# The attention's gate made token major, ahead of the other gate, and multiplied before the transposes

## The chip, the cores and the metric

One core of one Trainium2 chip runs the whole program. The time is the device time of one execution in microseconds (us). The engines are TensorE (PE in the profile, its weight loads PEld), VectorE (DVE), ScalarE (ACT), GpSimd (POOL) and SyncE (SP), whose queue issues every DMA of this kernel.

## The reference

One layer of a hybrid decoder trunk for 1024 tokens of width 1024, all in float32:

```python
z = rms_norm(h, mix_norm) @ w_in
q, k, v, gate_a, u, gate_s = split(z, 512 columns each)
attn = dilated_mixture_attention(q, k, v) * silu(gate_a)     # 8 heads of 64
ssm  = s5_glu(u, ...) * silu(gate_s)                         # 32 groups of 16 channels
h = h + concat(attn, ssm) @ w_out
h = h + sigmoid(rms_norm(h, ple_norm) @ w_g) * (p @ w_p)
```

The norm's gain is folded into x (`xh`, `xl`), and its factor per token, 1/rms, is applied where a projection leaves PSUM.

## The kernel before, in words

x is held feature major (channels on partitions, tokens along the row), `xh[k]` and `xl[k]` for the eight k tiles of 128 channels. Each float32 product is made of three matmuls of a high and a low part (`mm3`, lines 107 to 109): hi by hi, hi by lo, lo by hi. A weight tile of 128x512 is loaded by `load_w` (152), its high part is made by ScalarE (157) and its low part by VectorE or GpSimd (158). There are eight buffers for high parts and eight for low parts (`nbuf=8`), so the weights of one section of `w_in` replace those of the section before it as its last matmuls are done, and three buffers for raw tiles.

1/rms is there in two forms: `rrow`, spread over partitions and running along the row (for feature-major results), and `rcol`, one column per block of 128 tokens (for token-major results).

The work in order: u (six tiles, then two), the statistics, the state space heads (`ssm_kernels`, `ssm_scan`, `ssm_out`, `ssm_store`, lines 497 to 614), the two gates (632 to 642), q and k (694 to 731), then v, the attention, the GLU and half of the output projection, woven into each other by `step` (842), which runs the generator `attention` (754) on by one or two heads at a time, then the attention's half of the output projection and the embedding gate. The order of the instructions on each engine isn't that of the source: a list scheduler lays them out at build time by priority and by estimated durations and due times. `tc.high_priority` moves a block ahead. In the run each engine and the SP queue take their instructions strictly in that order. The gates' matmuls thus lie between those of the state space heads.

**The gates before.** For gate_s (columns 2560 on), then for gate_a (1536 on), eight weight tiles are loaded, and `feat_tile` (450) makes eight feature-major tiles of 128 channels by 512 tokens in the two `big` banks of PSUM, 24 matmuls each. VectorE multiplies a tile by `rrow` out of PSUM (640), ScalarE applies SiLU in place (641), SP stores it (642) into `sg_s` or `sa_s` in DRAM, both [512, 1024] feature major.

**The end of an attention block before** (`output`, 757 to 767). The attention's result for the 128 tokens of block b is `atok`, token major, evicted by VectorE (835) into one of two buffers (`wa`). `output(b)` loads the gate's 128 channels by 4 by 128 tokens into `gl` (tile `ga`, one buffer: `GA = 1`, line 760), transposes `atok` by four matmuls with the identity into a `t` bank (763; two such banks), multiplies by the gate on VectorE out of PSUM into `gl` (764), and splits that (`split`, 735 to 737) into a high part `mah` on ScalarE and a low part `mal` on GpSimd (`EA = "QQ"`, Q is GpSimd). `gl` comes free when the low part is done. The blocks 0, 1, 4 and 5 are held back (`HOLD`): their `output` is written down with that of block 2 and of block 6. `mah` and `mal` take buffers that the GLU's inputs held, so the first of them can be written only when the GLU is nearly done.

`tok_tiles` (648) makes token-major tiles (128 tokens by 512 channels; x is the stationary operand, w the moving one), before for q, k and v only.

Of the kernel before, what the change touches and what calls it, by code (L numbers as in the profile page):

```python
# [15 lines left out]
OP = mybir.AluOpType  # L16
# [61 lines left out]
def hybrid_layer(ctx: ExitStack, tc: tile.TileContext, a: dict, dbg=None):  # L78
# [22 lines left out]
    sg_s = dr.tile([512, S], F32, name="sg_s")  # L101
    sa_s = dr.tile([512, S], F32, name="sa_s")
    yg_s = dr.tile([512, S], F32, name="yg_s")
# [20 lines left out]

# [1 line left out]
    wp = ctx.enter_context(tc.tile_pool(name="wp", bufs=4, side="right"))  # L126
# [106 lines left out]

# [1 line left out]
    def p16(name):  # L235
# [136 lines left out]

    # powers of A: PA = [Re; -Im], PB = [-Im; -Re]
    pa, pb = named("pa", (P, G, 9)), named("pb", (P, G, 9))
# [43 lines left out]

    # rotations e^{i 8 theta k}, k = 16 a + b; sine rows are [s; -s]
    e1c, e1s = csr, snr  # L420
# [37 lines left out]
    def ev(name, shape=(P, 512)):  # L458
        return rp.tile(list(shape), F32, tag="ev", name=name, bufs=4)
# [171 lines left out]

# [1 line left out]
    for c0, dst in ((2560, sg_s), (1536, sa_s)):  # L633
        w = [load_w(wp, a["w_in"], k, c0, lo=GL) for k in range(KT)]
        for f in range(4):
            for n in range(2):
                o = feat_tile(w, f, n, "big", f"g{c0}{f}{n}")
                gt_ = ev(f"gate{c0}{f}{n}")
                with tc.high_priority(offset=AHEAD):
                    V.tensor_tensor(gt_, o, rrow[:, n * 512:(n + 1) * 512], op=OP.mult)  # L640
                    A.activation(gt_, gt_, AF.Silu)
                nc.sync.dma_start(dst[f * P:(f + 1) * P, n * 512:(n + 1) * 512], gt_)

    rrp.close()

# [1 line left out]
    kvp = ExitStack()  # L647
    def tok_tiles(w, bs, names, tag):
# [5 lines left out]
        return os_  # L654

    at = kvp.enter_context(tc.tile_pool(name="at", bufs=1))
    ph2 = ExitStack()
# [36 lines left out]
    for which, c0 in (("q", 0), ("k", 512)):  # L694
        w = [load_w(wp, a["w_in"], k, c0) for k in range(KT)]
        for bp in range(4):
# [19 lines left out]
            for b in (2 * bp, 2 * bp + 1):  # L716
# [10 lines left out]
                else:  # L727
# [3 lines left out]
                    nc.sync.dma_start(ks[:, :, c], hl, transpose=True)  # L731
# [1 line left out]
    ma, ms_ = {}, {}  # L733
# [20 lines left out]
    def attention():  # L754
        held = []

        def output(b):
            n, at_ = b // 4, atok.pop(b)
            gl = b3[0].tile([P, 4, P], F32, tag="ga", name=f"ga{b}", bufs=GA)
            nc.sync.dma_start(gl, sa_s.rearrange("(r p) t -> p r t", p=P)[:, :, b * P:(b + 1) * P])  # L760
            tp = bank("t", f"at{b}").rearrange("p (r t) -> p r t", t=P)
            for j in range(4):
                T.transpose(tp[:, j], at_[:, j], ident)
            tt(gl, tp, gl, OP.mult)
            if n not in ma:
                ma[n] = quad(f"mah{n}"), quad(f"mal{n}")
            split(*(t_[:, b % 4] for t_ in ma[n]), gl.rearrange("p r t -> p (r t)"), E[EA[b % 2]])

# [107 lines left out]

# [1 line left out]
    rawp[0] = ctx.enter_context(tc.tile_pool(name="raw2", bufs=RAW[1], side="right"))  # L878
# [43 lines left out]

# [1 line left out]
    def out_proj(part, src, scale, done):  # L924
# [124 lines left out]
def _w_in_columns():  # L1049
    """The u section with the channels of a group ahead of its groups."""  # L1050
    n = np.arange(3072)
    n[2048:2560] = n[2048:2560].reshape(4, 8, 16).transpose(0, 2, 1).reshape(512)
    return n
# [72 lines left out]
```

## Time and profile before

| | |
|---|---|
| time, median of 3 runs | 690.49 us (690.44 to 690.92) |
| span of the profiled execution, first to last instruction | 686.2 us |
| own time of the profiled execution | not given; the median lies 4.3 us above its span |
| mean granted TensorE clock | 0.968 |
| busy: PE, DVE, ACT, POOL | 630.0, 496.8, 289.5, 302.0 us |
| chain that ended last | PE 46%, DVE 26%, DMA 12%, issue 7%, ACT 5% |

A share over the whole span is a mean over stages with different limits. The stages here: u and the statistics to about 62 us, the state space heads with the gates' matmuls between them from 62 to 222 us, q, k and v to about 376, attention with GLU and output projection to 520, and the dense end. In the timeline an item's busy time may overlap the next one's; the distance of the starts is what an instruction takes out of its engine's time.

### The profile page before, as it was taken

How to read it: one execution, taken by the hardware profiler on the slowest of the kernel's cores; microseconds unless marked ns; L12 is line 12 of the kernel's file. 1: busy time of each engine (PE TensorE's matmuls, PEld its weight loads, DVE VectorE, ACT ScalarE, POOL GpSimd, SP SyncE). 2: the span in 40 equal slices, each digit the busy share in tenths (PEclk: the TensorE clock that was granted, in tenths of full speed). 3: DMA queues.
4: the chain of work that ended last, by engine and by line, in shares of the span. 5: the costliest groups of instructions: out<-in, count | busy, mean ns of one | idle time of the engine just before them, and what ended most of it. 6: DMA issues, size and time to landing. Idle time of an engine off the chain costs nothing.

```text
span 686.2 us, 10942 instructions
## 1 busy us (share of the span) xinstructions
PE 630.0 (92%) x3836; PEld 491.9 (72%) x3836; DVE 496.8 (72%) x1126; ACT 289.5 (42%) x553; POOL 302.0 (44%) x230
## 2 busy tenths in 40 slices
PE   9997799777879999999899789889999999999997
PEld 6875577566768788877677556566677888888786
DVE  6999999899998557767553998957944766626322
ACT  7532123445576624348434646534513455113100
POOL 3433825866775224234332845422432437342641
PEclk9999899998999999999999889989999999999999
DMA  7803612323444746754661868899987243015101
GB/s 257 241 7 109 209 38 76 105 79 93 77 92 92 167 69 125 159 86 125 161 122 48 216 147 148 213 192 191 217 226 244 94 152 124 15 63 165 50 32 61
DMA packets 158119, 87.25 MB, mean 127 GB/s; under 512 B 117232, under 2 KB 130416, under 8 KB 158064
## 3 DMA queue, kind: packets, MB, share of 16 engines
q1 hardware_dynamic: 158064, 86.56, 50.7%
q8 instruction: 30, 0.49, 0.3%
q14 instruction: 25, 0.20, 0.1%
HBM read 48.81 MB, written 17.27 MB: 96 GB/s over the span
## 4 chain that ended last, share of the span: by engine, by line
PE 46%; DVE 26%; DMA 12%; issue 7%; ACT 5%; POOL 2%; SPq 1%; DVEq 0%; ACTq 0%; POOLq 0%
PE gt L108 4%; PE gt L109 4%; PE gt L107 3%; DMA wr<-in_w_in 3%; DMA pt<-hl 3%; PE oa L107 2%; PE oa L109 2%; PE oa L108 2%; DVE tmp L270 2%; PE q L109 2%; PE q L107 2%; PE q L108 2%; DVE wl L158 2%; DVE p L780 2%; PE k L108 2%
## 5 line engine op out<-in xcount | busy, mean ns | idle before, releaser
L158 POOL TENSOR_TENSOR wl<-wr,wh 128x512 fp32r<-128x512 f32 x34 | 49.4, 1457 | 67.8 <-ACT wh L157 44.5
L157 ACT ACTIVATE wh<-wr 128x512 fp32r<-128x512 f32 x68 | 41.9, 626 | 51.4 <-DMA wr<-in_w_in 22.4
L810 POOL TENSOR_TENSOR hl<-p,hl 128x384 f16<-128x384 f32 (+2 forms) x34 | 38.9, 1148 | 53.9 <-ACT hl L807 27.1
L107 PE MATMUL g<-xh,wh 128*128 128x512 f32 x128 | 52.6, 411 | 7.3 <-DVE gate L640 5.5
L109 PE MATMUL g<-xh,wl 128*128 128x512 f32 x128 | 52.5, 410 | 5.3 <-DVE wl L158 5.3
L803 ACT ACTIVATE p<-p,st 128x384 f32<-128x384 f32 (+4 forms) x64 | 39.8, 622 | 39.1 <-DVE st L780 38.9
L108 PE MATMUL g<-xl,wh 128*128 128x512 f32 x128 | 52.0, 407 | 0.0
L108 PE MATMUL gt<-hl,wh 128*128 128x512 f32 (+1 forms) x136 | 51.7, 381 | 0.0
L107 PE MATMUL gt<-hh,wh 128*128 128x512 f32 (+1 forms) x136 | 51.7, 382 | 0.0
L109 PE MATMUL gt<-hh,wl 128*128 128x512 f32 (+1 forms) x136 | 51.2, 382 | 0.0
L158 DVE TENSOR_TENSOR wl<-wr,wh 128x512 fp32r<-128x512 f32 x34 | 34.8, 1025 | 19.1 <-ACT wh L157 14.0
L1016 ACT ACTIVATE gg<-gg 128x512 f32<-128x512 f32 (+1 forms) x17 | 10.1, 605 | 67.4 <-DVE gg L270 67.2
L1018 POOL TENSOR_TENSOR gg<-gg,hs 128x512 f32<-128x512 f32 x14 | 18.0, 1290 | 43.1 <-DVE gg L270 41.5
L107 PEld LDWEIGHTS g<-xh,wh 128*128 128x128 f32 x128 | 24.6, 192 | 13.7 <-DVE gate L640 6.5
L270 DVE TENSOR_TENSOR gg<-gt,rrow 128x512 f32<-128x512 f32 (+1 forms) x17 | 10.8, 656 | 32.7 <-PE gt L109 32.6
L109 PEld LDWEIGHTS g<-xh,wl 128*128 128x128 f32 x128 | 24.7, 193 | 12.0 <-DVE wl L158 6.6
L818 PE MATMUL pv<-vv,pt 128*128 128x64 f16 x504 | 24.4, 198 | 6.3 <-DMA pt<-hl 6.2
L818 PEld LDWEIGHTS <-pt 128*128 128x128 f16 x504 | 19.0, 101 | 14.8 <-DMA pt<-hl 8.9
L107 PEld LDWEIGHTS gt<-hh,wh 128*128 128x128 f32 x136 | 25.6, 188 | 5.5
L108 PEld LDWEIGHTS gt<-hl,wh 128*128 128x128 f32 x136 | 25.6, 188 | 5.4
L109 PEld LDWEIGHTS gt<-hh,wl 128*128 128x128 f32 x136 | 25.6, 188 | 5.4
L780 DVE CUSTOM_DVE_ANT_0 p<-sc,mask,gc 128x128 f32<-128x128 f32 (+3 forms) x56 | 24.3, 458 | 6.7 <-PE sc L793 3.2
(330 smaller groups left out, 1957.2 us busy)
## 6 DMA issues: line engine op xcount, KB each, us to landing
wr<-in_w_in SPq DMA_DIRECT2D x48, 256.0 KB, 2.9
xr<-in_x SPq DMA_DIRECT2D x16, 256.0 KB, 4.7
wr<-in_w_out SPq DMA_DIRECT2D x16, 256.0 KB, 3.3
xos<-in_x SPq DMA_DIRECT2D x16, 256.0 KB, 4.0
h_s<-xos SPq DMA_DIRECT2D x16, 256.0 KB, 3.4
xoa<-h_s SPq DMA_DIRECT2D x16, 256.0 KB, 2.8
wr<-in_w_ple_gate SPq DMA_DIRECT2D x16, 256.0 KB, 3.0
out_t<-gg SPq DMA_DIRECT2D x15, 256.0 KB, 2.0
```

The costliest lines, as they stand in the source:

```text
L107: T.matmul(o, lh, rh, start=first, stop=False)
L108: T.matmul(o, lh, rl, start=False, stop=False)
L109: T.matmul(o, ll, rh, start=False, stop=last)
L157: A.activation(hi, raw, AF.Copy)
L158: E[lo_on[k % len(lo_on)]].tensor_tensor(lo, raw, hi.bitcast(F32), op=OP.subtract)
L270: V.tensor_tensor(o, x, y, op=op)
L780: V.tensor_tensor_reduce(out, sc, msk, gm, init, op0=OP.add, op1=OP.min, accum_out=acc_[:, hd:hd + 1])
L803: A.activation(pb_, pb_, AF.Exp, bias=mx[:, hc], scale=-1.0, accum_out=dn[:, hc])
L810: E[LE[b][h0 % len(LE[b])]].tensor_tensor(hl[:, na:2 * na], pr_[:, 0:na], hl[:, 0:na], op=OP.subtract)
L818: T.matmul(pv[:, hd], pt[:, nf + i * nt + j + na * lp, :], vv[:, k0 + j, hd, lv, :], start=first, stop=end and not nf and j == n - 1 and l ...
L1016: A.activation(gt_, gt_, AF.Sigmoid)
L1018: (V if last else Q).tensor_tensor(gt_, gt_, hs, op=OP.add)
```

## The change

gate_a is computed first, gate_s second. gate_a is made token major by `tok_tiles` (blocks 0 and 1 together, then one at a time) and leaves PSUM by one ScalarE instruction, SiLU with `rcol` as its scale per partition; `sa_s` becomes [8, 128, 512], one contiguous block per 128 tokens. In `output`, `gl` is loaded as 128 rows of 512 values, GpSimd multiplies it onto `at_` in place, the product is transposed, and the split reads PSUM: the high part on ScalarE, the low part now on VectorE. gate_s is as before apart from its place. The rest of the diff takes comments out.

```diff
-    sa_s = dr.tile([512, S], F32, name="sa_s")
+    sa_s = dr.tile([NB, P, 512], F32, name="sa_s")
...
-    for c0, dst in ((2560, sg_s), (1536, sa_s)):
-        w = [load_w(wp, a["w_in"], k, c0, lo=GL) for k in range(KT)]
-        for f in range(4):
-            for n in range(2):
-                o = feat_tile(w, f, n, "big", f"g{c0}{f}{n}")
-                gt_ = ev(f"gate{c0}{f}{n}")
-                with tc.high_priority(offset=AHEAD):
-                    V.tensor_tensor(gt_, o, rrow[:, n * 512:(n + 1) * 512], op=OP.mult)
-                    A.activation(gt_, gt_, AF.Silu)
-                nc.sync.dma_start(dst[f * P:(f + 1) * P, n * 512:(n + 1) * 512], gt_)
...
+    w = [load_w(wp, a["w_in"], k, 1536, lo=GL) for k in range(KT)]
+    for bs in ((0, 1), (2,), (3,), (4,), (5,), (6,), (7,)):
+        for b, o in zip(bs, tok_tiles(w, bs, [f"ga{b}" for b in bs], "big")):
+            gt_ = ev(f"gate_a{b}")
+            with tc.high_priority(offset=AHEAD):
+                A.activation(gt_, o, AF.Silu, scale=rcol[:, b:b + 1])
+            nc.sync.dma_start(sa_s[b], gt_)
+    w = [load_w(wp, a["w_in"], k, 2560, lo=GL) for k in range(KT)]
+    for f in range(4):
+        for n in range(2):
+            o = feat_tile(w, f, n, "big", f"gs{f}{n}")
+            gt_ = ev(f"gate_s{f}{n}")
+            with tc.high_priority(offset=AHEAD):
+                V.tensor_tensor(gt_, o, rrow[:, n * 512:(n + 1) * 512], op=OP.mult)
+                A.activation(gt_, gt_, AF.Silu)
+            nc.sync.dma_start(sg_s[f * P:(f + 1) * P, n * 512:(n + 1) * 512], gt_)
...
-            nc.sync.dma_start(gl, sa_s.rearrange("(r p) t -> p r t", p=P)[:, :, b * P:(b + 1) * P])
+            nc.sync.dma_start(gl, sa_s[b].rearrange("p (r t) -> p r t", r=4))
+            E[EA[b % 2]].tensor_tensor(at_, at_, gl, op=OP.mult)
             tp = bank("t", f"at{b}").rearrange("p (r t) -> p r t", t=P)
             for j in range(4):
                 T.transpose(tp[:, j], at_[:, j], ident)
-            tt(gl, tp, gl, OP.mult)
             if n not in ma:
                 ma[n] = quad(f"mah{n}"), quad(f"mal{n}")
-            split(*(t_[:, b % 4] for t_ in ma[n]), gl.rearrange("p r t -> p (r t)"), E[EA[b % 2]])
+            split(*(t_[:, b % 4] for t_ in ma[n]), tp.rearrange("p r t -> p (r t)"), V)
```

## Rows read from the trace of the kernel before

**Rows 1.** The page's first two parts: the span, each engine's busy time, share of it and instructions, and PE's busy share in 40 equal slices of 17.2 us, in tenths.

```profile
span 686.2 us, 10942 instructions
PE 630.0 (92%) x3836; PEld 491.9 (72%) x3836; DVE 496.8 (72%) x1126; ACT 289.5 (42%) x553; POOL 302.0 (44%) x230
...
PE   9997799777879999999899789889999999999997
```

**Rows 2.** Busy time of each engine by stretch, for the state space stage. Columns: stretch and its length in us, busy us (instructions) of each engine, granted clock, DMA share, GB/s.

```profile
60.00:76.00 16.00, 14.26 (x63) 12.19 (x64) 14.48 (x63) 3.48 (x6) 8.87 (x8) 0.89 0.52 161
76.00:81.00 5.00, 0.85 (x4) 0.41 (x3) 5.00 (x17) 0.32 (x1) 3.50 (x5) 0.76 0.72 216
81.00:128.00 47.00, 46.94 (x227) 37.19 (x226) 44.14 (x132) 14.85 (x42) 21.68 (x17) 0.95 0.27 85
128.00:152.00 24.00, 15.68 (x82) 12.17 (x81) 23.39 (x24) 10.82 (x17) 20.55 (x14) 1.00 0.28 94
152.00:222.00 70.00, 59.41 (x326) 49.04 (x327) 66.80 (x89) 42.10 (x75) 46.27 (x31) 0.95 0.43 89
```

**Rows 3.** What PE waited for from 60 to 240 us. Columns: us in total, times, longest.

```profile
PE g L107 <- DVE gate L640: 5.5, 2, 4.2
PE g L109 <- DVE wl L158: 5.3, 3, 3.0
```

**Rows 4.** PE's timeline around the first two gate tiles. Columns: start, us, instruction, idle before it and what ended that.

```profile
76.12 0.40 PE L109 MATMUL g<-xh,wl 128*128 128x512 f32 x1
80.67 0.80 PE L107 MATMUL g<-xh,wh 128*128 128x512 f32 x1 [4.15 <-DVE gate L640]
...
85.51 0.39 PE L109 MATMUL g<-xh,wl 128*128 128x512 f32 x1
85.73 0.40 PE L107 MATMUL g<-xh,wh 128*128 128x512 f32 x1
```

**Rows 5.** Groups of instructions from 60 to 240 us. Columns: line, engine, operation, output and inputs, shapes, count, busy us and mean ns, idle time before them.

```profile
L640 DVE TENSOR_TENSOR gate<-g,rrow 128x512 f32<-128x512 f32 x16 | 10.9, 680 | 0.0
L641 ACT ACTIVATE gate<-gate 128x512 f32<-128x512 f32 x16 | 10.1, 632 | 39.6 <-DVE gate L640 39.5
L525 ACT ACTIVATE gt<-gp 128x512 f32<-128x512 f32 x8 | 4.7, 587 | 1.2 <-PE gp L523 1.1
```

**Rows 6.** VectorE's timeline around three of the gates' multiplications, and the last scan of the state space heads.

```profile
79.94 0.68 DVE L640 TENSOR_TENSOR gate<-g,rrow 128x512 f32<-128x512 f32 x1
...
81.00 1.66 DVE L509 TENSOR_TENSOR g<-g,gw 128x512 f32<-128x512 f32 x1
...
117.93 0.68 DVE L640 TENSOR_TENSOR gate<-g,rrow 128x512 f32<-128x512 f32 x1
118.53 0.95 DVE L563 TENSOR_TENSOR es<-es,ex 128x512 f32<-128x512 f32 x1
...
134.31 0.68 DVE L640 TENSOR_TENSOR gate<-g,rrow 128x512 f32<-128x512 f32 x1
...
135.51 1.82 DVE L270 TENSOR_TENSOR xpv<-xpv,ysw 128x508 f32<-128x508 f32 x1
...
218.07 1.36 DVE L578 TENSOR_TENSOR_SCAN y<-r,w 128x128 f32<-128x128 f32 x4
```

**Rows 7.** The same stretches as in rows 2, for the attention stage.

```profile
376.00:400.00 24.00, 19.27 (x115) 12.34 (x113) 24.00 (x36) 15.59 (x33) 19.22 (x15) 0.86 0.77 195
400.00:420.00 20.00, 16.85 (x182) 12.62 (x182) 18.25 (x45) 9.84 (x23) 7.61 (x8) 0.83 0.79 162
420.00:440.00 20.00, 16.38 (x224) 11.18 (x223) 20.00 (x47) 11.43 (x27) 11.83 (x9) 0.93 0.76 167
440.00:460.00 20.00, 18.05 (x225) 12.01 (x224) 12.69 (x43) 7.36 (x18) 5.33 (x5) 0.84 1.00 210
460.00:480.00 20.00, 19.66 (x257) 14.09 (x256) 15.64 (x50) 9.78 (x24) 5.89 (x5) 0.98 0.93 184
480.00:500.00 20.00, 18.88 (x284) 13.08 (x283) 18.62 (x44) 9.80 (x20) 8.63 (x6) 1.00 1.16 209
500.00:520.00 20.00, 18.91 (x167) 14.58 (x166) 8.03 (x12) 5.07 (x8) 6.14 (x5) 1.00 0.84 240
```

**Rows 8.** VectorE's groups from 376 to 520 us, shapes kept apart.

```profile
L737 DVE TENSOR_TENSOR msl<-ym,msh 128x512 fp32r<-128x512 f32 x8 | 8.4, 1047 | 0.0
L270 DVE TENSOR_TENSOR ga<-at,ga 128x512 f32<-128x512 f32 x8 | 5.5, 688 | 9.1 <-DMA ga<-sa_s 9.1
```

**Rows 9.** GpSimd's groups from 376 to 520 us.

```profile
L917 POOL TENSOR_TENSOR ym<-ym,gm 128x512 f32<-128x512 f32 x8 | 11.1, 1386 | 16.0 <-DMA gm<-sg_s 6.8 <-DVE hl L809 6.7 <-PE glu L109 1.7
L737 POOL TENSOR_TENSOR mal<-ga,mah 128x512 fp32r<-128x512 f32 x8 | 11.0, 1372 | 22.2 <-ACT mah L736 22.2
```

**Rows 10.** The SP queue's timeline, two of the eight loads of the attention's gate (start, us that the queue took to issue it).

```profile
376.42 0.43 SPq L760 DMA_DIRECT2D ga<-sa_s  x1
...
444.27 0.39 SPq L760 DMA_DIRECT2D ga<-sa_s  x1
```

**Rows 11.** A piece of the chain that ended last (start, us, what the chain ran through).

```profile
444.27 5.76 DMA ga<-sa_s
```

**Rows 12.** DMA issues: KB each, median us from issue to landing.

```profile
ga<-sa_s SPq DMA_DIRECT2D x8, 256.0 KB, 3.9
gm<-sg_s SPq DMA_DIRECT2D x8, 256.0 KB, 3.0
```

More of the change, by code (lines that the diff above doesn't have):

```diff
@@ L630, in hybrid_layer @@
     sp.close()
-    for c0, dst in ((2560, sg_s), (1536, sa_s)):
-        w = [load_w(wp, a["w_in"], k, c0, lo=GL) for k in range(KT)]
-        for f in range(4):
-            for n in range(2):
-                o = feat_tile(w, f, n, "big", f"g{c0}{f}{n}")
-                gt_ = ev(f"gate{c0}{f}{n}")
-                with tc.high_priority(offset=AHEAD):
-                    V.tensor_tensor(gt_, o, rrow[:, n * 512:(n + 1) * 512], op=OP.mult)
-                    A.activation(gt_, gt_, AF.Silu)
-                nc.sync.dma_start(dst[f * P:(f + 1) * P, n * 512:(n + 1) * 512], gt_)
-    rrp.close()
-    kvp = ExitStack()
     def tok_tiles(w, bs, names, tag):
@@ L654, in tok_tiles @@
         return os_
+    w = [load_w(wp, a["w_in"], k, 1536, lo=GL) for k in range(KT)]
[14 more added lines that the diff above has]
+            nc.sync.dma_start(sg_s[f * P:(f + 1) * P, n * 512:(n + 1) * 512], gt_)
+    rrp.close()
+    kvp = ExitStack()
     at = kvp.enter_context(tc.tile_pool(name="at", bufs=1))
```

## The prediction

> **What bounds the kernel now.** I read the engine totals first [rows 1]. PE is busy 92% of the span, so time can go only where PE idles or runs at its lower clock, and the total doesn't say where that is. The view by stretch says it. In the state space stage PE idles 1.7 us of 60 to 76, 4.15 of 76 to 81, almost nothing of 81 to 128, 8.3 of 128 to 152 and 10.6 of 152 to 222; VectorE is busy 44.1 of 47, 23.4 of 24 and 66.8 of 70 us in the last three [rows 2]. So the first gate's half is paced by PE after a hole at its start, and the rest of the stage by VectorE, with the gates' matmuls as PE's filler. The waits name the hole: PE waited 5.5 us for the gate's multiplication on VectorE, 4.2 of them at once, and 5.3 us for the low parts of weights [rows 3]. In the timeline the hole lies between the second and third tile: both `big` banks are full at 76.5, VectorE comes to the first at 79.94 because its queue holds other work, and PE goes on at 80.67 at half rate: of its next matmuls the twelfth starts at 85.51, so 11 steps take 0.44 us each, where the step after them is 0.22 [rows 4, 6]. The granted clock of that stretch is 0.76, a mix of the two levels [rows 2].
>
> In the attention stage PE is busy 128.0 of 144 us. VectorE is full from 376 to 400 and from 420 to 440, then has room, and the DMA share stands at about 1 from 440 to 500 [rows 7]. VectorE stood 9.1 us in five waits for the load of the attention's gate [rows 8], and one of these loads, 5.76 us long, is on the chain that ended last [rows 11]. From there on PE is busy nine tenths in every slice but the last [rows 1], and the change touches nothing.
>
> **The change part by part.** The times shown have no figure for the profiled execution itself, so I sum against the median, 690.49 us, which is 4.3 above the span of 686.2; I take those 4.3 us as unchanged.
>
> *Eviction of gate_a.* Eight multiplications leave VectorE. Each takes 0.68 us busy, but the next instruction starts 0.60 us after it (117.93 to 118.53) [rows 5, 6], so VectorE gets back 8 x 0.60 = 4.8 us. ScalarE still runs eight SiLU, now out of PSUM. The nearest row for a 128x512 read of PSUM is 587 ns against 632 for the gate's SiLU from SBUF [rows 5]; it is no longer, and ScalarE is busy 14.9 of 47 us [rows 2], so I cost it at nothing. If that cover were gone it would be 8 x 0.63 = 5.1 us on ScalarE. The new wait is ScalarE on PE; behind it in ScalarE's queue stand the copies for the state space heads and the weights' high parts. It stood 39.5 us in waits for VectorE's multiplication before [rows 5], so this wait replaces a longer one.
>
> *The order.* The first section is now the one without VectorE. Its first two tiles can be evicted as they end, at 76.5 instead of 80.6. Of the 4.15 us hole some 0.7 stay (one SiLU before the first bank is free), and the half rate after it, 11 x (0.44 - 0.22) = 2.4 us, should go with it: PE is ahead by 4.15 - 0.7 + 2.4 = 5.8 us at 128. That isn't added to the 4.8: from 128 on VectorE paces, so the stage ends earlier by what VectorE is ahead. The second section's weights can't load before the first section's last matmuls; those waits (5.3 us) [rows 3] move forward and stay. Matmuls and weight loads of PE keep their number, and gate_s as second section does what gate_a did there. The eight stores are 256 KB as before, on the SP queue; behind each of them stand the next section's weight loads, and a store now waits for ScalarE alone. Zero.
>
> From 223 us on, in q, k and v, PE's slices stand at nine tenths seven times running and at eight once [rows 1], so what the stage gains is kept: **-4.8 us**. Bounds: 0 if the freed slots become waits, -5.8 if PE's lead holds.
>
> *The end of an attention block.* VectorE loses a multiplication out of PSUM (0.69) and gets the low part out of PSUM, the same two operand places, same size: zero. GpSimd loses the low part (1.37 mean) and gets a multiplication SBUF by SBUF, priced by the GLU's gate product, 1.39 [rows 8, 9]: 8 x 0.02, zero. ScalarE reads PSUM instead of SBUF: zero as above. The load has rows of 2 KB instead of 512 bytes; the load of the other gate, with 2 KB rows, lands in 3.0 us against 3.9 [rows 12], 0.9 less each, on a queue where the DMA engines are full. The one `gl` buffer comes free after GpSimd's product instead of at the end of the split, so the next load can start a whole block earlier; before, the first load was issued at 376.42 and a later one at 444.27, on the chain [rows 10, 11]. VectorE's 9.1 us of waits should mostly go. What is late next is `xos` and the transposed probabilities, since PE idles only 1.95 us in the slice of that load and 4.5 us from 440 to 520 [rows 7].
>
> Against it: the transposes now wait for load and product, and behind them in PE's queue stand the GLU's and the output projection's matmuls. A product takes 1.39, so the latency per block is longer ahead of PE and shorter behind it by the same. Behind the product on GpSimd stand the probabilities' low parts; behind VectorE's low part, which waits for ScalarE's high part, stand the row minima. That last pattern exists eight times in the GLU (`msl` after `msh`) without a wait in its row [rows 8]. The two `t` banks are held until the low part instead of until the product; only the attention uses them there. This part is worth between -4.5 (all of PE's idle time after 440) and +20.2 us (if PE takes over VectorE's 9.1 us of waits and all eight products, 8 x 1.39 = 11.1). I take **-1.0**, half of the 1.95 us that PE idled in the slice of the load on the chain, because PE is near its limit there.
>
> Sum: 690.5 - 4.8 - 1.0 = **684.7 us**.
>
> **A rule weighed.** VectorE instructions with two inputs in SBUF are stretched where GpSimd runs (1.66 and 1.82 us at 81.00 and 135.51), while the gate's multiplication, with one input in PSUM, takes 0.68 at every place shown [rows 6]. The Trainium skill, "SBUF — State Buffer", section "SBUF: two separate sides", says that VectorE with two SBUF inputs and GpSimd take a shared pair of ports by an exclusive lock, for a whole instruction. By that rule a multiplication taken out just ahead of a stretched instruction gives nothing back. The rows agree with the lock in direction; how it decides for this change is the third rival.
>
> **The rivals.**
>
> *Both leads add up.* The state space stage keeps PE's 5.8 us, and the attention stage gives its whole 4.5: 690.5 - 10.3 = 680.2. For it: 9.1 us of VectorE waits and the single buffer. Against: VectorE's 66.8 of 70 us. Chance 0.13.
>
> *No change.* VectorE's freed slots turn into waits for GpSimd and ScalarE, and the scheduler's new order costs what is left. For it: between 128 and 152 GpSimd is busy 20.6 of 24 us [rows 2]. Against: VectorE's own 94 to 98%. 690.5, chance 0.08.
>
> *The freed slots are swallowed.* Three multiplications stand close ahead of a stretched instruction (79.94, 117.93, 134.31) [rows 6]. If VectorE then only blocks 0.6 us longer there, five of eight count: 5 x 0.60 = 3.0, and 690.5 - 3.0 - 1.0 = 686.5. Chance 0.15.
>
> *PE waits in the attention stage (slower).* PE's queue is fixed by estimates, and the loads were later than estimated: VectorE stood at them [rows 8]. If the scheduler sets the transposes as soon as it believes the product done, PE inherits the lateness, where VectorE took it before; and the products of blocks 0 to 3 move into 376 to 430, where VectorE is full and is stretched by GpSimd. Place: the eight `output` calls, 380 to 515.  Price up to 20.2; the point from which it decides is 4.8 us, a quarter of that. At three eighths, 7.5 us, the time is 690.5 - 4.8 + 7.5 = 693.2. Against it: the loads can run a block ahead. Chance 0.19.
>
> **How the numbers follow.** The forecast, 684.7 with 681.5 to 688 of its own (0 to -5.8 and what rescheduling of the whole program may add or take), has 0.45. Faster: 0.45 + 0.13 + 0.15 = 0.73; same 0.08; slower 0.19. The bound is 0.2%, 1.4 us, about what a measurement can tell here. The range that holds 8 in 10 takes in the first rival but its lower tail and the milder half of the slow one: 679.0 to 692.0.
>
> **What would show it.** Right: no hole in PE's timeline at 76 us and full rate after it; the state space heads' last scan on VectorE about 5 us earlier than 218.07 [rows 6]; only eight gate multiplications on VectorE; the loads of the attention's gate issued a block ahead, and VectorE's waits for them near zero. Wrong: PE waiting for GpSimd at the transposes; VectorE's idle time between 128 and 222 up by 3 us or more; a granted clock under 0.83 anywhere from 376 to 440.

## The result and the profile after

| | before | after |
|---|---|---|
| time, median | 690.47 us (688.24 to 690.92, 4 runs) | 699.94 us (694.42 to 700.48, 4 runs) |
| span of the profiled execution | 686.2 us | 698.7 us |
| mean granted TensorE clock | 0.968 | 0.957 |

The ratio is 1.0132, with a 95% interval of 1.009 to 1.0175: the change made the kernel slower by some 9 us (6 to 12). The forecast was 684.7, faster, with 679.0 to 692.0 as its range; sign and range were both missed. One kernel's runs lie up to 9 us apart here (e6), so a difference below whose interval takes in zero is said to do so. The two profiled executions are one run each and lie 12.5 us apart, more than the medians: the changed kernel's is its slowest of four, and the time of every run for which both are known lies 1.7 to 1.9 us above its span, so the span of 686.2 belongs to a run of some 688 us, below the median.

The page's totals of the kernel after: span, busy time by engine, PE by 40 slices.

```profile
span 698.7 us, 10923 instructions
PE 634.3 (91%) x3836; PEld 495.7 (71%) x3836; DVE 492.8 (71%) x1118; ACT 292.1 (42%) x554; POOL 302.5 (43%) x230
...
PE   9997599878789999999999598879897999999997
```

Eight VectorE instructions are gone and VectorE is busy 4.0 us less than in [rows 1]; PE does the same 3836 matmuls in a span 12.5 us longer. What counts is where PE idles more. Five marks in PE's timeline say it. They are the starts of the last matmul of a kind, in us:

| last matmul of | before | after | difference |
|---|---|---|---|
| q | 270.8 | 274.6 | +3.8 |
| v | 374.0 | 375.4 | +1.4 |
| the GLU | 425.0 | 433.3 | +8.3 |
| the output projection's first half (`os`) | 520.2 | 528.1 | +7.9 |
| the embedding gate | 681.1 | 693.6 | +12.5 |

**The state space stage.** The stretches that answer to [rows 2] (columns as there):

```profile
60.00:76.00 16.00, 13.75 (x55) 11.78 (x56) 15.32 (x66) 3.48 (x6) 8.91 (x8) 0.79 0.56 172
76.00:81.00 5.00, 2.30 (x10) 1.51 (x8) 5.00 (x17) 1.97 (x2) 3.18 (x3) 1.00 0.77 227
81.00:128.00 47.00, 41.38 (x202) 33.41 (x203) 40.66 (x127) 12.52 (x37) 20.61 (x17) 0.89 0.24 75
128.00:152.00 24.00, 18.40 (x83) 14.15 (x82) 23.30 (x22) 12.06 (x20) 22.22 (x15) 0.86 0.27 88
152.00:222.00 70.00, 59.60 (x330) 48.64 (x329) 65.23 (x88) 42.30 (x74) 44.62 (x30) 0.98 0.51 94
```

VectorE is relieved as forecast (149.5 us busy over the five rows, 153.8 before), but PE did 5.6 us less from 81 to 128, at a clock of 0.89 for 0.95. PE's timeline (start, us, instruction, idle before it) shows why:

```profile
77.90 0.40 PE L109 MATMUL ga<-wh,xl 128*128 128x512 f32 x1
86.62 1.09 PE L523 MATMUL gp<-ident,g 128*128 128x128 f32 x4 [8.33 <-issue]
```

The hole at 78 us is not gone: it is 8.33 us long, where it was 4.15 [rows 4]. In PE's fixed order the transposes of the state space kernel (`gp`) now stand ahead of the third gate tile, and what they transpose, `g`, comes late on VectorE. VectorE's timeline (start, us, instruction):

```profile
81.19 1.24 DVE L270 TENSOR_TENSOR ebc<-ebc,tmp 128x128 f32<-128x128 f32 x1
82.35 1.24 DVE L270 TENSOR_TENSOR ebs<-ebs,tmp 128x128 f32<-128x128 f32 x1
...
85.84 0.68 DVE L509 TENSOR_TENSOR g<-g,gw 128x512 f32<-128x512 f32 x1
```

Before, `g` stood 1.06 us behind the gate's multiplication, at 81.00 [rows 6], and `ebc` and `ebs` came after it; with the multiplication gone the scheduler put `ebc`, `ebs` and others ahead of it. The profile calls the wait "issue", but it ends 0.1 us after `g` does (85.84 + 0.68). In q, k and v PE catches up, so that 1.4 us are left at the end of v.

**The attention stage.** Its stretches, to hold against [rows 7]:

```profile
376.00:400.00 24.00, 15.55 (x93) 9.85 (x93) 22.76 (x33) 13.96 (x31) 21.70 (x17) 0.84 0.75 195
400.00:420.00 20.00, 18.41 (x191) 13.54 (x190) 20.00 (x40) 10.26 (x22) 9.12 (x7) 0.93 0.78 173
420.00:440.00 20.00, 16.05 (x197) 11.30 (x198) 20.00 (x49) 11.43 (x27) 10.77 (x9) 0.91 0.66 143
440.00:460.00 20.00, 17.60 (x229) 12.42 (x228) 17.52 (x50) 9.90 (x25) 7.02 (x7) 1.00 0.91 201
460.00:480.00 20.00, 16.71 (x278) 10.67 (x280) 14.24 (x41) 7.32 (x17) 5.03 (x4) 0.83 1.05 187
```

From 376 to 400 PE is busy 15.55 us for 19.27, GpSimd 21.70 for 19.22. SP issued four of the gate's loads by 411 us (start, us); before, the second was issued at 434.30:

```profile
377.82 0.42 SPq L766 DMA_DIRECT2D ga<-sa_s  x1
383.67 0.38 SPq L766 DMA_DIRECT2D ga<-sa_s  x1
396.03 0.44 SPq L766 DMA_DIRECT2D ga<-sa_s  x1
411.14 0.57 SPq L766 DMA_DIRECT2D ga<-sa_s  x1
```

So the products of blocks 0 to 3 now run at 381.4, 390.2, 409.4 and 426.2, in the GLU's stage; before, one multiplication ran there, at 382.05, and the next at 439.94. What held them back before was the one `gl` buffer. The first block's product lay in it until its high part could be written, over the GLU's inputs, after `ym` had read them; the next load went out behind that:

```profile
428.75 0.63 ACT L736 ACTIVATE mah<-ga 128x512 fp32r<-128x512 f32 x1 [0.86 <-DVE ym L915]
434.30 0.38 SPq L760 DMA_DIRECT2D ga<-sa_s  x1
```

Now `gl` is free when GpSimd's product ends, and the product waits in place for its transposes. PE's longest wait in the changed kernel's GLU stage, and VectorE's timeline ahead of it:

```profile
389.86 0.59 PE L799 MATMUL sc<-ks,qh 128*128 128x512 f16 x1 [4.83 <-DVE st L786]
```

```profile
383.12 1.71 DVE L815 CAST hl<-p 128x384 f16<-128x384 f32 x2
384.75 1.40 DVE L743 TENSOR_TENSOR ygl<-yl,ygh 128x512 fp32r<-128x512 f32 x1
386.26 1.21 DVE L921 TENSOR_TENSOR ym<-ygh,ygl 128x512 f32<-128x512 f32 x1
387.39 1.75 DVE L743 TENSOR_TENSOR ygl<-yl,ygh 128x512 fp32r<-128x512 f32 x1
389.06 0.74 DVE L786 CUSTOM_DVE_ANT_0 p<-sc,mask,gc 128x512 f32<-128x512 f32 x1
```

The same place before:

```profile
381.51 0.62 DVE L809 CAST hl<-p 128x384 f16<-128x384 f32 x2
382.05 0.68 DVE L270 TENSOR_TENSOR ga<-at,ga 128x512 f32<-128x512 f32 x1
382.65 0.83 DVE L737 TENSOR_TENSOR ygl<-yl,ygh 128x512 fp32r<-128x512 f32 x1
383.40 1.40 DVE L915 TENSOR_TENSOR ym<-ygh,ygl 128x512 f32<-128x512 f32 x1
384.72 0.61 DVE L780 CUSTOM_DVE_ANT_0 p<-sc,mask,gc 128x384 f32<-128x384 f32 x1
```

Two things changed for the row minimum that gives PE its bank back. The casts and `ygl` ahead of it are longer (1.71 for 0.62, 1.40 for 0.83) while GpSimd runs almost without a gap, and one more `ygl` of 1.75 us stands ahead of it. PE's waits there were 2.19 and 1.21 us before.

**The attention's half of the output projection.** At 539.80 PE waits 2.75 us for an eviction (`xoa`), which it didn't before. SP's queue around the end of `os`, after:

```profile
526.61 0.33 SPq L941 DMA_DIRECT2D xoa<-h_s  x1
526.99 0.42 SPq L957 DMA_DIRECT2D h_s<-xos  x1
530.71 0.32 SPq L941 DMA_DIRECT2D xoa<-h_s  x1
531.07 0.43 SPq L957 DMA_DIRECT2D h_s<-xos  x1
531.61 0.90 SPq L152 DMA_DIRECT2D wr<-in_w_out  x2
```

and before:

```profile
519.24 0.94 SPq L935 DMA_DIRECT2D xoa<-h_s  x2
520.28 0.38 SPq L951 DMA_DIRECT2D h_s<-xos  x1
520.76 0.85 SPq L152 DMA_DIRECT2D wr<-in_w_out  x2
```

The last two weight tiles were issued 0.5 us after the last `os` matmul began (520.22) before, and 3.5 us after it (528.10) now. They stand behind a reload of h that waits for one of the four `ev` buffers, a ring that it shares with the stores of h. On ScalarE and VectorE these weights' parts (537.46 on VectorE) stand ahead of the second eviction (539.07), which is how a late load reaches PE.

### The profile page after: what moved, and what is told of

It is laid out like the page before. It is cut to its first block, busy times and chain, and to the rows that moved or that the text cites. A ratio compares the mean times of both kernels' runs of the same rounds, so it can differ in the third digit from the quotient of the medians.

```text
span 698.7 us, 10923 instructions
## 1 busy us (share of the span) xinstructions
PE 634.3 (91%) x3836; PEld 495.7 (71%) x3836; DVE 492.8 (71%) x1118; ACT 292.1 (42%) x554; POOL 302.5 (43%) x230
## 4 chain that ended last, share of the span: by engine, by line
PE 48%; DVE 18%; DMA 16%; issue 8%; ACT 5%; POOL 4%; SPq 1%; DVEq 0%; ACTq 0%; POOLq 0%
DMA pt<-hl 6%; PE gt L108 3%; PE gt L109 3%; PE gt L107 3%; PE q L109 2%; PE q L107 2%; PE q L108 2%; DMA wr<-in_w_in 2%; DMA wr<-in_w_out 2%; PE oa L107 2%; PE oa L109 2%; PE oa L108 2%; PE k L108 2%; PE k L109 2%; PE k L107 2%
## 5 line engine op out<-in xcount | busy, mean ns | idle before, releaser
L158 DVE TENSOR_TENSOR wl<-wr,wh 128x512 fp32r<-128x512 f32 x34 | 32.0, 943 | 30.0 <-ACT wh L157 28.7
L815 DVE CAST hl<-p 128x384 f16<-128x384 f32 (+2 forms) x34 | 24.0, 707 | 15.5 <-DMA pt<-hl 11.7
L107 PE MATMUL gs<-xh,wh 128*128 128x512 f32 x64 | 27.2, 425 | 2.6 <-ACT wh L157 2.6
L107 PE MATMUL os<-msh,wh 128*128 128x512 f32 x64 | 27.3, 427 | 2.4 <-DVE xos L281 2.4
L109 PE MATMUL gs<-xh,wl 128*128 128x512 f32 x64 | 26.7, 417 | 3.0 <-DVE wl L158 1.7
L107 PE MATMUL oa<-mah,wh 128*128 128x512 f32 x64 | 26.2, 409 | 2.8 <-DVE xoa L281 2.8
L978 POOL TENSOR_TENSOR ssb<-ssb,xoa 128x512 f32<-128x512 f32 x12 | 15.8, 1315 | 29.0 <-ACT xoa L977 29.0
```

Source lines behind the costliest of these rows:

```text
L107: T.matmul(o, lh, rh, start=first, stop=False)
L109: T.matmul(o, ll, rh, start=False, stop=last)
L158: E[lo_on[k % len(lo_on)]].tensor_tensor(lo, raw, hi.bitcast(F32), op=OP.subtract)
L815: V.tensor_copy(hl[:, 0:na], pr_[:, 0:na])
L978: E[SB2[f]].tensor_tensor(ssb[:, c], ssb[:, c], xr, op=OP.add)
```

## The experiments

Each ratio is against runs of the kernel before on the same chip in the same group, with its 95% interval. "1% = 6.9 us" turns it into time.

### First group: which part

**e1, the gates alone.** The end of a block as before, with `sa_s` replaced by `sg_s` in its load:

```diff
-            nc.sync.dma_start(gl, sa_s[b].rearrange("p (r t) -> p r t", r=4))
-            E[EA[b % 2]].tensor_tensor(at_, at_, gl, op=OP.mult)
+            nc.sync.dma_start(gl, sg_s.rearrange("(r p) t -> p r t", p=P)[:, :, b * P:(b + 1) * P])
...
+            tt(gl, tp, gl, OP.mult)
```

> The gates as in the changed kernel (gate_a first, token major, evicted by ScalarE alone), the end of an attention block as in the kernel before; there it loads the other gate's array, which has the layout that the old code reads, so the attention's result is multiplied by gate_s. Theory A (the loss has two sources; the gates cost 1.4 us by the end of v, the end of an attention block costs some 8 us behind it): a hole of about 8 us on PE near 78 us as in the changed kernel, the last start of v near 375.4, then GLU and output projection as before, time 690.5 + 1.4 = 692 us (690 to 694). Rival B (the new place of the gates reshuffles the whole program, and the stages behind inherit it; the new end of a block is free): time about 699, with the 7 us between 375 and 433 present.

Measured: 1.0026 (1.0001 to 1.0051), +1.8 us. The hole is there (9.2 us at `gp`), v ends at 374.9, the GLU at 425.1.

**e2, the end of a block alone.** The kernel before with the new `output`, its load reading `sa_s.rearrange("(b q) (h c) -> b (q h) c", b=8, h=2)[b]`.

> The gates as in the kernel before, in their old order and feature major; only the end of an attention block is changed (product on GpSimd ahead of the transposes, split out of PSUM, load of one contiguous block; it reads the same bytes as 8 blocks of 128 x 512, so the values of the gate are permuted). Theory A: no hole at 78 us, last start of v at 374.0 as before, then +7 us between 375 and 433 and perhaps +4 in the attention's output projection: 697 to 701 us. Rival B: 690.5 within 1.5 us.

Measured: 1.0133 (1.009 to 1.0177), +9.2 us. At 78 us PE waits 3.2 us for the gate's multiplication, as in the kernel before (4.15), and 0.3 us at `gp`; the GLU ends at 430.3, `os` at 526.8, and PE waits 3.3 us for `xoa`.

**e3, the order alone.**

```diff
-    for c0, dst in ((2560, sg_s), (1536, sa_s)):
+    for c0, dst in ((1536, sa_s), (2560, sg_s)):
```

> The kernel before with its two gate sections swapped, both feature major and evicted by VectorE and ScalarE; nothing else. If the order of the sections alone makes the hole at the transposes of the state space kernel, PE idles about 8 us near 78 us here too and the time is 691 to 693. If the hole comes from the pair of token-major tiles and its eviction, this is the kernel before: a hole of about 4.2 us at 76.5 and 690.5 within 1.5 us.

Measured: 0.999 (0.997 to 1.0011). The order by itself costs nothing.

**e4, gate_a second.** The two sections of the changed kernel swapped, nothing else.

> The changed kernel with its two gate sections swapped back: gate_s first, then gate_a, still token major and evicted by ScalarE alone. If the place of the ScalarE eviction makes the hole at 78 us, it shrinks to the 4.2 us of before, VectorE's work on the state space heads still loses eight multiplications, and v ends up to 4.8 us ahead of the changed kernel's 375.4; the rest keeps its 8 us: 694 to 699. If token-major tiles cost time wherever they stand, 699 to 702.

Measured: 1.0112 (1.0069 to 1.0154), +7.7 us. The wait at `gp` is 0.3 us. Against e2, which has the old gates, that is -1.5 us by the ratios, with intervals that overlap, where -4.8 was forecast; in the traces v ends at 374.6, in e2 at 373.7.

What follows: theory A holds in its first half. The loss is the end of a block; the new gates cost 1.8 us (an interval of 0.1 to 3.5) and give nothing; rival B falls.

### Second group: what in the end of a block

**e5, no product.**

```diff
-            E[EA[b % 2]].tensor_tensor(at_, at_, gl, op=OP.mult)
```

> The changed kernel without the multiplication by the attention's gate (the gate is still made, stored and loaded); transposes, split out of PSUM and everything else stay. GpSimd loses eight products, and the transposes wait for nothing but the attention's result. On VectorE the order near 385 us is that of before again (the row minimum for which PE waits stands straight behind ym), and SP issues the last weights of the output projection ahead of the reloads of h as before. Theory A1 (the product on GpSimd does it, by lengthening and reordering what VectorE does from 380 to 400, and the last weights come late behind it): no PE wait over 3 us near 385, no PE wait at 539, 689 to 693. Theory A2 (the split out of PSUM with its low part on VectorE and the two t banks held from 382 to 435 do it): 697 or more.

Measured: 0.9983 (0.9957 to 1.0008): the whole loss is gone, 10.3 us below the changed kernel. Load, transposes, the split out of PSUM and `mal` on VectorE cost nothing that shows without the product; `mal` takes 0.68 us there, and A2 falls. But e5 does less work than any kernel that applies the gate. Against e1, with the same gates and the old end of a block, it is 3.0 us lower by the ratios, so up to that much of the 10.3 may be the price of the products wherever they stand.

**e6, the product beside the path.**

```diff
-            E[EA[b % 2]].tensor_tensor(at_, at_, gl, op=OP.mult)
+            E[EA[b % 2]].tensor_tensor(gl, at_, gl, op=OP.mult)
```

> The changed kernel, but GpSimd's product goes into the gate's own buffer and the transposes read the attention's result without it (the output lacks the gate): the same work on GpSimd, the same order on VectorE as in the changed kernel, but PE's transposes no longer wait for the load and the product. Theory A1 (the product's place on GpSimd and VectorE's order behind it): still a PE wait of 4 to 5 us at the scores near 389, time 696 to 700. Rival C (PE inherits the latency of load and product at the transposes, the rival of the prediction): the loss goes, 689 to 692.

Measured: 1.016 (1.0099 to 1.0222). The first transposes run at 352.5 us again and wait for no product, and the loss stays, with a PE wait of 5.1 us at the scores. Rival C falls: it isn't the latency that PE inherits. Nor is it that the product holds one of the two `atok` buffers longer: from 374 to 430 PE waits 0.8 us for an `atok` eviction in the changed kernel, 0.2 in e6 and not at all in e7.

**e7, the product on VectorE** (`EA = "VV"`).

> The changed kernel with the product on VectorE (8 x about 0.6 to 1.2 us more there, 8 x 1.35 less on GpSimd); transposes still wait for it. On VectorE the row minimum near 385 stands straight behind ym again, as before; on SP the last weights of the output projection stand behind three reloads of h instead of two. Theory A1: the wait near 389 shrinks to 2 to 3 us and the GLU stage gains 3 to 5 us on the changed kernel, while the wait for the first xoa near 539 stays or grows by one reload (up to 2 us): 693 to 698. Rival C: nothing gained, 698 to 702.

Measured: 1.013 (1.0091 to 1.017). The wait at the scores shrinks to 2.9 us, as A1 said; but one of 4.1 us for the GLU's tanh takes its place, and the gain of 3 to 5 us that A1 expected didn't come. So it isn't GpSimd as such: on VectorE a product takes 1.11 us in that stage, and the loss is the same.

**e8, reloads on another queue.**

```diff
-                  nc.sync.dma_start(xr, src[f * P:(f + 1) * P, c])
+                  (nc.sync if part == "s" else Q).dma_start(xr, src[f * P:(f + 1) * P, c])
```

> The changed kernel with the reloads of h (xoa) issued on GpSimd's queue, so that the last weights of the output projection no longer stand behind them on SP. The engines' order of work up to 520 us is that of the changed kernel. Theory D (the late weights behind the reload cost the 4.3 us of the attention's output projection): no PE wait at 539.8, oa shorter by 3 to 5 us, 695 to 697. If the reload only happened to stand there and the weights wait for their buffers: 699 to 702.

Measured: 1.0137 (1.01 to 1.0173), and PE waits 3.7 us for `xoa`. It tells nothing on theory D: on GpSimd's queue the reload at 524.17 waited 3.1 us, the low part of a weight stood behind it, and the last weights were issued at 526.04, 5.3 us after the last `os` matmul.

### Third group: which products, and is VectorE's time the reason

**e9 and e10, no product for the blocks 0 to 3, and for 4 to 7.**

```diff
-            E[EA[b % 2]].tensor_tensor(at_, at_, gl, op=OP.mult)
+            if b > 3: E[EA[b % 2]].tensor_tensor(at_, at_, gl, op=OP.mult)
```

> The changed kernel without the multiplication by the gate for the blocks 0 to 3 (their products fell into 379 to 425, in the GLU stage); the products of blocks 4 to 7 stay. Theory A3 (four products moved into the stage where VectorE is full from 376 to 430, and cost about what they lengthen there): the GLU's last matmul is back near 426 to 428 and the time at 688 to 693, all but 1 to 3 us of the loss gone. Theory E (the late blocks do it, whose product stands between the last attention matmuls and the attention's output projection): still 697 or more.

> The changed kernel without the multiplication for the blocks 4 to 7; those of 0 to 3 stay. Theory A3: the GLU's last matmul stays near 433 and the time at 695 to 700. Theory E: 688 to 692.

Measured: e9 1.0054 (1.0031 to 1.0078), e10 1.0103 (1.007 to 1.0136). Against the changed kernel's 1.0132 the first four products cost 5.4 us, the last four 2.0, and the latter's intervals overlap. The 5.4 has an interval of some 2 to 9. E falls. A3's numbers were missed, too: in e9 the GLU ends at 430.6, not at 426 to 428, and the time, 694.2 by the ratio, lies just above the range. Like e5, e9 leaves work out; it doesn't put it back where it stood. In e9 the wait for `xoa` is still there (3.1 us).

**e11 and e12, `ym` by DMA, on the changed kernel and on the one before** (`RY = "D"`).

> The changed kernel with the GLU's own input (ym) loaded again by DMA instead of added up by VectorE from its high and low part: eight adds of 1.07 to 1.25 us leave VectorE between 380 and 430, eight loads of 256 KB join SP's queue. Theory A3 (VectorE's time from 376 to 430 is what the products took): the GLU stage gains 4 to 8 us, 692 to 696. If the stage is bound by something else (SP's queue, the loads), 699 or more.

> The kernel before with the same edit as the control. If VectorE is the bound of the GLU stage there too, 685 to 688; if the stage has slack on VectorE before the change, or the eight loads cost as much, 689 to 692.

Measured: e11 1.0132 (1.0097 to 1.0167), e12 1.0008 (0.9985 to 1.0032). VectorE was relieved (50.5 us busy of 374 to 430, for 53.0), and nothing was won. A3's "VectorE's time from 376 to 430 is what the products took" is not borne out in this form. The edit isn't clean, since it adds eight loads: PE's waits for the transposed probabilities from 376 to 440 grew from 2.0 to 4.7 us in e11. In the traces the last `os` matmul does start earlier than without the edit (525.4 for 528.1, and 517.8 for 520.2), and e12 loses that again behind it.

### What the stretch 374 to 430 shows over all kernels

One row each (columns as in [rows 2]). The kernel before, the changed one, e5 and e7:

```profile
374.00:430.00 56.00, 46.95 (x445) 32.18 (x443) 53.87 (x105) 34.18 (x74) 35.84 (x28) 0.88 0.75 167
```

```profile
374.00:430.00 56.00, 43.65 (x392) 30.25 (x390) 52.97 (x93) 30.61 (x65) 37.44 (x28) 0.88 0.75 178
```

```profile
374.00:430.00 56.00, 46.57 (x423) 32.10 (x422) 54.05 (x107) 34.59 (x75) 35.78 (x26) 0.91 0.92 208
```

```profile
374.00:430.00 56.00, 43.67 (x408) 30.02 (x407) 51.71 (x99) 31.04 (x67) 32.94 (x24) 0.88 0.83 178
```

| kernel | products of 0 to 3 here | PE busy of 56 us | wait for `xoa` |
|---|---|---|---|
| before | no | 46.95 | none |
| e1 | no | 46.71 | 0.8 |
| e5 | no | 46.57 | 0.7 |
| e9 | no | 45.25 | 3.1 |
| e12 | no | 45.47 | 3.6 |
| after | yes | 43.65 | 2.75 |
| e2 | yes | 43.58 | 3.3 |
| e6 | yes | 43.59 | 3.0 |
| e7 | yes (VectorE) | 43.67 | 3.7 |
| e10 | yes | 43.33 | 3.0 |
| e11 | yes | 43.58 | 0.9 |

The other kernels fit: e4, e8, e13 and e16, with the products, have 43.4 to 44.7; e3, e14, e15, e17 and e18, without, 45.0 to 47.8. PE loses 2.6 us in this stretch (43.57 for 46.19, the means of the table) wherever the four products lie in it, on GpSimd or VectorE, with or without PE waiting for them. (In the kernels with the old end of a block the first of the four lies there already, on VectorE.) That is about half of the 5.4 us that they cost; the rest comes later and wasn't placed. The wait for `xoa` doesn't follow them: e12 has it without any change to the attention and e11 has 0.9. It needed an experiment of its own.

### Last two groups: the late weights

**e13 and e14, own buffers for the reloads of h**, on the changed kernel and on the one before.

```diff
-                xr = ev(f"xo{part}{f}{n}")
+                xr = ev(f"xo{part}{f}{n}") if part == "s" else hp.tile([P, 512], F32, tag="xo", name=f"xo{part}{f}{n}", bufs=4)
```

> The changed kernel with the reloads of h (xoa) in four buffers of their own instead of the ring that they share with the stores of h (the space comes free as the attention ends); PE's order is that of the changed kernel, VectorE's nearly. In the changed kernel the last pair of weights of the output projection was issued 3.5 us after the projection's first half ended, behind a reload that waited for a ring buffer; in the kernel before 0.5 us after it. Theory D: the last weights are issued within 1 us of the end, no PE wait of 3 us for xoa, the attention's output projection shorter by 3 to 4 us, 694 to 697. If the weights themselves are late (their raw buffers, the high and low parts) the wait stays: 698 to 701.

> The control: the kernel before with the same four buffers. It had no PE wait for xoa, so Theory D expects no difference: 689 to 691.5. A gain of over 2 us here would mean that the edit is worth something by itself and not for what the change did.

Measured: e13 1.0134 (1.0098 to 1.0171), e14 1.006 (1.0037 to 1.0083). Both went against Theory D's numbers, and e14 then says the most for it: the edit made the good kernel worse by 4.1 us. SP's queue in e14, whose last `os` matmul starts at 519.69, and PE's wait after it:

```profile
522.38 0.33 SPq L989 DMA_DIRECT2D pr<-in_p  x1
522.80 0.86 SPq L152 DMA_DIRECT2D wr<-in_w_out  x2
```

```profile
PE oa L107 <- DVE xoa L281: 3.3, 1, 3.3
```

The load of p (`pr`, line 989) uses the same ring and had moved ahead of the last weights: issued 3.1 us after the end of `os`, a wait of 3.3 us. In e13 it took the reload's place in the same way (weights 3.0 us late, wait 2.7).

**e15, e9 and e13 together.**

> Both at once: the changed kernel without the products of blocks 0 to 3 and with own buffers for the reloads. If the loss is the sum of these two, the time is that of the kernel before with the new gates: 688 to 691.5. If something else is left it is 693 or more.

Measured: 1.0061 (1.0036 to 1.0085): like e9, since own buffers for the reloads alone don't bring the weights forward.

**e16 and e17, the loads of p in own buffers too; e18, that with no product for blocks 0 to 3.**

```diff
-            pr_ = ld(f"pr{k}{n}")
+            pr_ = hp.tile([P, 512], F32, tag="xo", name=f"pr{k}{n}", bufs=4)
```

> The changed kernel with the reloads of h and the loads of p both in own buffers. In the run before this one the reload no longer stood ahead of the last weights, but the load of p did, which took its place at the same ring; the last weights were again 3.0 us late. Now no load that waits for the ring stands ahead of them, only stores of h. Theory D: last weights issued within 1.5 us of the end of the first half, no PE wait of 2 us or more for xoa, 694 to 696.5. If the lateness comes from the raw buffers or the stores of h, the wait stays and the time is 697 to 700.

> The control on the kernel before. With the reloads alone in own buffers it became slower (692.6 against 689.1): there too the load of p came to stand ahead of the last weights, which were issued 3.1 us after the end of the first half instead of 0.5, and PE waited 3.3 us for xoa. Theory D: with p moved as well that wait is gone and the time is back at 688 to 690.5. If the new place of the buffers is what costs, it stays at 692 or more.

> The changed kernel without the products of blocks 0 to 3 and with own buffers for the reloads of h and for p. If the loss is the sum of the products in the GLU stage and the late last weights, 688.5 to 691.5 is what is left; 693 or more says that a third cause is in it.

Measured: e17 0.9999 (0.9982 to 1.0015): e14's 4.1 us are back, with the last weights 1.2 us after the end and a wait of 1.6 us. e16 1.0114 (1.009 to 1.0138): the weights are 0.9 us late and the wait for `xoa` is gone, but the time fell by 1.2 us only, within the intervals, where at least 3.4 was expected; PE waits 2.9 us for an `xos` eviction in `os` instead (1.5 in the changed kernel). e18 1.0041 (1.0014 to 1.0069), +2.8 us, of which e1 has 1.8; that is more than the expectation left for the two causes alone.

One more reading of the traces, one execution of each kernel, shows where the late weights count: the time from the start of the last `os` matmul to the end of the span.

| kernels | PE's wait for `xoa` | from the last `os` to the end, us |
|---|---|---|
| after, e2, e6 to e10, e12 to e14 | 2.7 to 3.7 | 168.8 to 173.4, mean 170.8 |
| before, e1, e3 to e5, e11, e15 to e18 | 0 to 1.9 | 165.6 to 168.2, mean 166.8 |

The kernel before has 166.0 there, the changed one 170.6, e16 166.2. So of the 12.5 us between the two profiled executions 4.6 lie behind `os` and 7.9 ahead of it, and e16 takes back what lies behind. What e16, e17 and e18 lose lies ahead: their last `os` matmul starts 1.3, 2.7 and 2.0 us later than in the changed kernel, the one before and e9, which lack only the own buffers. No run shows why.

What follows: a load that waits for the ring, in front of the last weights, makes the wait of about 3 us. In the kernel before that is worth 4 us, put in and taken out again (e14, e17), and over all kernels the part behind `os` is 4 us longer with it. In the changed kernel the wait is there and can be taken out, but of the whole time little comes back, since that edit delays `os`. With the two causes taken out, what is left is the gates' 1.8 us and 1.0 us that the intervals don't tell from nothing. No version here is measurably faster than the kernel before.

## Why the prediction was wrong

- **"VectorE gets back 8 x 0.60 = 4.8 us", "-4.8 us".** VectorE's busy time did fall by 4.3 us, but the last scan moved from 218.07 [rows 6] to 216.86, by 1.2 us. The step that failed is "from 128 on VectorE paces, so the stage ends earlier by what VectorE is ahead": a busy share of 95% was read as a bound, but most of the time given back became idle time, and PE was hardly busier from 152 to 222 than before (59.60 us for 59.41):

```profile
216.86 1.35 DVE L578 TENSOR_TENSOR_SCAN y<-r,w 128x128 f32<-128x128 f32 x4
```

The new hole on PE isn't the reason, since in e4, without it, that scan starts at 217.10. That it is a chain over several engines that paces the heads is the likely reading; no run took it apart. It was the forecast's bound of 0, and e1 fell on its other side (+1.8). In e4 the ratio leaves 1.5 us at its middle, and v doesn't end earlier.
- **"Some 0.7 stay", "PE is ahead by ... 5.8 us".** The hole grew to 8.33 us. The wait that was removed was not the only one there: the transposes of `g` had stood behind the third tile, and the new order has them ahead of it. The text asked "what is late next" in the attention stage and not here.
- **ScalarE out of PSUM is "no longer".** The SiLU takes 686 ns for 632 before [rows 5]; 8 x 0.05 us on an engine with room. Wrong, and without weight.
- **The order at zero.** Right (e3).
- **"The end of an attention block ... -1.0."** +9.2 (e2). The single terms were well priced: `mal` on VectorE 0.68, the product on GpSimd 1.31 mean (1.39 forecast), load to landing 3.5 us, loads issued a block ahead, VectorE's waits for them gone. What failed is "8 x 0.02, zero": GpSimd's exchange was priced as if the new instruction stood where the old one had. The text saw that the `gl` buffer comes free earlier, "a whole block earlier", and counted it as a gain alone. For blocks 1 to 3 the multiplication stands 34 to 50 us earlier, where VectorE is busy 22.8 of 24 us and GpSimd 21.7, and then VectorE all the time to 440; without the first four products 5.4 us come back (e9). The buffer had held the multiplications back to a stage with room, at the price of VectorE's waits [rows 8]. That the earlier place makes the loss, and not the product's new form, is argued from this and from the table of 374 to 430; no run puts the new products back to the old times.
- **The slow rival** (693.2, chance 0.19) joined two mechanisms. "PE inherits the lateness" is refuted (e6). "The products of blocks 0 to 3 move into 376 to 430" is what happened (e9, e10, and the table). Its price of three eighths, 7.5 us, was near the end of a block's 9.2, by luck: it was worked out from the waits and products that PE would take over, the half that is refuted. The 4.8 set against it weren't there.
- **The signs.** None of the three signs of being wrong came: PE waits for no product at the transposes (its one wait there, 1.5 us at 438.03, is for a low part that frees a `t` bank), VectorE's idle time from 128 to 222 grew by 1.7 us, not 3, and the clock from 376 to 440 is 0.84 or more. It was the signs of being right that failed, the hole and the last scan. Those on the loads and on VectorE's waits for them came true, while the stage got slower.
- **The late weights** were in no part of the prediction. It bounded the attention stage and took the rest as untouched ("the change touches nothing" from there on); an order laid out anew moved a load in SP's queue, and the part behind `os` takes 4.6 us more.

What stays open: by which of the full engines the four products cost PE its time. GpSimd's part (e7), PE's wait for the product (e6) and some of VectorE's other work (e11) were taken out singly, and the loss stayed. Later and earlier products weren't tried.

## What to carry to other kernels

A buffer that comes free late can be holding work back to a place where it costs little: before removing the wait, ask into which stage the released work will move, and price it there, not by its duration alone. A 95% busy engine need not be the pace of its stage, and where a scheduler lays out the order, the next late operand takes the hole. Look last at what a shared ring of buffers puts ahead of the next stage's weights in the load queue: in e14 the order of one load was worth 4 us.

## What the runs showed of the hardware

VectorE's casts, which have one input in SBUF, are stretched where GpSimd is busy, and not only its two-input operations. Two casts of 128x512 in the changed kernel: the first runs while GpSimd stands idle, the second starts 0.10 us into a product and ends 0.28 us after it.

```profile
405.08 0.42 DVE L815 CAST hl<-p 128x512 f16<-128x512 f32 x1
...
409.36 1.27 POOL L767 TENSOR_TENSOR atok<-atok,ga 128x512 f32<-128x512 f32 x1
409.46 1.45 DVE L815 CAST hl<-p 128x512 f16<-128x512 f32 x1
```

The group of casts of 128x384 from 374 to 430 us, in the changed kernel and in e7, where the product is VectorE's (busy us, mean ns, idle):

```profile
L815 DVE CAST hl<-p 128x384 f16<-128x384 f32 x6 | 5.1, 857 | 0.0
```

```profile
L815 DVE CAST hl<-p 128x384 f16<-128x384 f32 x6 | 3.1, 530 | 2.1 <-DMA pt<-hl 2.1
```

The Trainium skill, "SBUF — State Buffer", section "SBUF: two separate sides", has VectorE operations in a two-port mode take the pair that GpSimd uses, too, as an exclusive lock; the second cast, which outlasts the product, fits such a lock, and no run here shows the port itself or the mode of the casts.
